# One set of four idle transposes in the gate and up products, where there were three

## The chip, the cores and the metric

The kernel runs on one core of one Trainium2 chip. The metric is the device time of one execution in microseconds (us); the time given for a kernel is the median of several runs.

## What is computed

One encoder block on 512 tokens of width 2048, all in float32: an adaptive norm, a combined input projection, two token mixers side by side (global attention and attention in a window), an output projection, and then a SwiGLU channel mixer with 5632 hidden features and a final norm. The change lies in the channel mixer:

```python
h2 = rms_norm(x, norm2_w[l]) * (1.0 + sc2) + sh2
ff = (jax.nn.silu(h2 @ w_ffn_gate[l]) * (h2 @ w_ffn_up[l])) @ w_ffn_down[l]
x = x + g2 * ff
return rms_norm(x, final_w)
```

## The kernel before

Every float32 product is made of three fp32r matmuls: each operand is split into a high part (ScalarE rounds it, line 135) and a low part (VectorE takes the difference, line 136), and `mm3` (lines 143 to 145) adds high x high, high x low and low x high in PSUM. TensorE's work is therefore a long line of weight loads (128x128) each followed by a matmul.

The program runs the input projection and both mixers first, then `w_out`, and from about 1244 us on the channel mixer, in three stages:

- **Gate and up.** The hidden features are worked in 11 groups of 512 (`for n in range(FU)`, line 1003), in each first `w_gate`, then `w_up`. Except for the first gate group, each is one call of `group7`: a Strassen-like scheme that forms four 512x512 blocks by seven products. It goes over the four blocks of the contraction in the order (2, 3, 0, 1). For each, `wforms` loads 1 MB of weights (SP's queue), makes their sums on VectorE (lines 875 to 878) and splits them into four `whl` tiles; then TensorE makes 84 matmuls of 128x256: seven products in the order 1, 2, 3, 5, 6, 7, 4 (`ORDER`), for each 2 x 2 x 3 matmuls. A group has 336 matmuls. At its end ScalarE and VectorE gather the seven PSUM banks into a tile `c` (lines 932 to 939), gate groups go through SiLU (line 1022), up groups are multiplied with them (line 1025) and stored in DRAM. The weights are prepared ahead of TensorE, by as much as the buffers (`raw`, `whl`) allow.
- **Down, 512 wide.** Two of the hidden groups go through `w_down` by plain products, 128x512 matmuls (about 2120 to 2207 us).
- **Down, 256 wide.** The other groups go through `down_group`, which again has seven products for most of them, with 128x256 matmuls (about 2207 to 2520 us), and a tail of 512-wide products with the final norm.

A *stir* is a call of `stirred` (line 842): four transposes of the 128x128 identity into a PSUM bank that nobody reads. They add nothing to the result. `keep_in_program_order` and `issue_after` (through `after_stir`) pin them: the next matmul of the program is not issued ahead of them. In `group7` a stir stands in front of the second block of the contraction, if the call's argument `stir` is set. Down groups have two of their own: in column block 0 at hidden group 2, and in column block 1 at hidden group 7. So before there are five stirs, 20 transposes: three in gate and up, two in down.

The order of the instructions on each engine is that of the program, with a scheduler that moves instructions by priority where nothing pins them.

Of the kernel before, what the change touches and what calls it, by code (L numbers as in the profile page):

```python
# [89 lines left out]
def encoder_block(ctx: ExitStack, tc, xp, xT, c, ada1_w, ada2_w, b_ada, norm1_w, w_in, q_norm_w, k_norm_w, bias,  # L90
# [33 lines left out]
    def bank(tag):  # L124
        return ps.tile([P, 512], F32, tag=tag, name=tag, bufs={"mm": 4, "S": 2, "T": 1, "Y": 1}[tag])
# [16 lines left out]
    def mm3(o, lh, ll, rh, rl, start, stop, **kw):  # L142
        nc.tensor.matmul(o, lh, rh, start=start, stop=False, **kw)  # L143
        nc.tensor.matmul(o, lh, rl, start=False, stop=False, **kw)  # L144
        nc.tensor.matmul(o, ll, rh, start=False, stop=stop, **kw)  # L145
# [696 lines left out]
    def stirred(b):  # L842

        for o in range(0, 4 * P, P):
            last = behind(nc.tensor.transpose(b[:, o:o + P], ident, ident))
        stir_last.append(last.ins)
# [3 lines left out]
    def after_stir():  # L850
        return tc.issue_after(stir_last.pop()) if stir_last else contextlib.nullcontext()
# [13 lines left out]
    def wforms(w, k0, c0, turned=False, late=False):  # L865
        rt = []
        for a in range(2):
            raw, r3 = unit(w, k0 + 2 * a, 2, c0, 512)
            rt.append((raw, r3[:, :, :256], r3[:, :, 256:]))
        (_, b11, b12), (r1, b21, b22) = rt  # L870
        ta = wq.tile([P, 1024], F32, tag="ta", name="ta", bufs=2)
        tb = wq.tile([P, 1024], F32, tag="tb", name="tb", bufs=1)
        t1, t2_ = (half(ta)[:, a] for a in range(2))
        t3, t4 = (half(tb)[:, a] for a in range(2))
        V.tensor_sub(t1, b12, b11)  # L875
        V.tensor_sub(t2_, b22, t1)  # L876
        V.tensor_sub(t3, b22, b12)
        V.tensor_sub(t4, *((b21, t2_) if turned else (t2_, b21)))
        hl = [wtiles() for _ in range(4)]
        col = lambda e: lambda t: t.rearrange("p (q n) -> p q n", q=2)[:, :, e * 256:(e + 1) * 256]  # L880
        blk = lambda e: lambda t: half(t)[:, e]
        g0 = [t[:, :512].rearrange("p (q n) -> p q n", q=2) for t in hl[0]]
        parts = (b11, (lambda t: t,)), (r1, (col(0), col(1))), (ta, (blk(0), blk(1))), (tb, (blk(0), blk(1)))
        turn = (0, 2, 3, 1) if late else range(4)
        return split7([parts[n] for n in turn], [g0] + hl[1:], [HALVES[n] for n in turn])
# [25 lines left out]
    def group7(wsrc, xs, order, dst, stir=False):  # L911

        bk = {r: bank(BANK[r]) for r in ORDER}
        for n, s in enumerate(order):
            w = wsrc(s)
            if stir and n == 1:
                tp = bank("T")
                stirred(tp)
            for r in ORDER:
                (wh, wl), (xh, xl) = w[r], xs[s][r]  # L920
                for q in range(2):
                    for c in range(2):
                        o = bk[r][:, c * 256:(c + 1) * 256]
                        cs = slice(c * P, (c + 1) * P)
                        first, last = n == 0 and q == 0 and c == 0, n == len(order) - 1 and q == 1
                        with after_stir():
                            mm3(o, wh[:, q, cs], wl[:, q, cs], xh[:, q], xl[:, q], first, last, skip_group_check=True)
        p = {r: b.rearrange("p (c n) -> p c n", c=2) for r, b in bk.items()}
        (d11, d12), (d21, d22) = dst
        with tc.high_priority():  # L930
            p1 = io.tile([P, 512], F32, tag="io", name="p1").rearrange("p (c n) -> p c n", c=2)
            S.activation(p1, p[1], AF.Copy)
            V.tensor_add(d11, p[2], p1)
            V.tensor_add(d21, p[6], p1)
            V.tensor_add(d12, p[5], d21)
            V.tensor_add(d12, p[3], d12)
            V.tensor_add(d21, p[7], d21)
            V.tensor_add(d22, p[5], d21)
            V.tensor_sub(d21, d21, p[4])
# [6 lines left out]
    hx = {}  # L946
# [38 lines left out]
    def c_tile(dt=F32, name="c"):  # L985
        n = next(cn) % 3
        c = (c_p if n else ca).tile([P, 2048], dt, tag=f"c{n}", name=name, bufs=1)
        return c, c.rearrange("p (a t q n) -> p a t q n", a=2, t=2, q=2)
# [9 lines left out]
    def first_pairs():  # L998
        early[0] = ff_pair(0, 0, [wq.tile([P, 1024], F32R, tag="ta", name=f"e0{t}", bufs=2) for t in "hl"], nc.sync)
        e1, _ = c_tile(F32R, "e1")  # L1000
        early[1] = ff_pair(0, 1, [e1[:, :1024], e1[:, 1024:]], nc.sync)

    for n in range(FU):
        cs = []
        for w in (w_gate, w_up):
            c, v = c_tile()
            cs.append(c)
            if n == 0 and w is w_gate:
                for f in range(4):
                    S.activation(v[:, f // 2, :, f % 2], banks[f].rearrange("p (t n) -> p t n", t=2), AF.Silu)  # L1010
                continue
            dst = (v[:, 0, 0], v[:, 1, 0]), (v[:, 0, 1], v[:, 1, 1])

            def wsrc(s):
                d = wforms(w, 4 * s, n * 512)
                if s == 1 and n == FU - 1 and w is w_up:
                    first_pairs()
                return d

            group7(wsrc, hx, (2, 3, 0, 1), dst, w is w_up and n < 3)  # L1020
            if w is w_gate:
                S.activation(c, c, AF.Silu)
        for a in range(2):
            sl = slice(a * 1024, (a + 1) * 1024)
            V.tensor_mul(cs[1][:, sl], cs[1][:, sl], cs[0][:, sl])
        (nc.sync if n < FU - 1 else nc.gpsimd).dma_start(ff_d[n], cs[1])
# [290 lines left out]
```

## Time and profile before

| | us |
|---|---|
| median of 3 runs | 2590.98 |
| lowest and highest run | 2590.06, 2592.19 |
| the profiled execution | 2587.8 |
| its span, first to last instruction | 2585.9 |
| TensorE busy | 2550.0 |
| VectorE busy | 1882.2 |
| ScalarE busy | 1024.5 |

The profile's names: PE is TensorE's matmuls, PEld its weight loads, DVE VectorE, ACT ScalarE, POOL GpSimd, SP SyncE, whose queue issues most loads of weights. A row of the timeline gives the start in us, the duration in us, engine, line, operation, the tile written and the tiles read, the shape, and the count of instructions merged into the row. Matmuls are pipelined: a 128x256 matmul lasts 0.28 us, but the next starts long before it ends, so the rate of work is read from starts, or from the count in a stretch of time, and not from durations. Tiles in the timeline: `whl` is a high or low part of weights, `m0` to `m7`, `x3` and `x56` are parts of the activations, `s` those of the down groups, `T`, `Y`, `S` and `mm` are PSUM banks. L845 is the transposes of a stir, L804 transposes that bring the activations into shape. The stirs of before start at 1303.89, 1380.51, 1457.12, 2211.72 and 2420.26 us.

### The profile page before, as it was taken

What the parts mean: (1) busy time and instruction counts of PE and PEld (TensorE: products, weight loads), DVE (VectorE), ACT (ScalarE), POOL (GpSimd) and SP (SyncE); (2) the same over time, 40 slices, a digit from 0 to 9 for tenths busy, and PEclk for the clock granted to TensorE, in tenths of its full rate; (3) what the DMA queues carried; (4) which work ended last, traced back from release to release, by engine and by line L of the source; (5) the groups of instructions that cost most, each with busy time, mean ns of one, the idle gap of its engine ahead of it and who ended that gap; (6) DMA issues with size and microseconds to landing.
All of it is one profiled execution on the core that took longest, in us unless ns stands there. A gap on an engine that the chain in (4) does not pass through costs nothing.

```text
span 2585.9 us, 40429 instructions
## 1 busy us (share of the span) xinstructions
PE 2550.0 (99%) x16525; PEld 2306.7 (89%) x16525; DVE 1882.2 (73%) x2500; ACT 1024.5 (40%) x1412; POOL 151.4 (6%) x254
## 2 busy tenths in 40 slices
PE   7999999999999999999999999999999999999998
PEld 5888888888888788888999999999999998999996
DVE  8985776456566566556788888787888885777877
ACT  5223554224233332235744444444444454434333
POOL 0100000111111110011000000000000000000010
PEclk8999999999999999999999999999999999999999
DMA  9864234765656876676443343343443446547563
GB/s 353 303 226 145 66 98 166 244 191 169 193 178 198 282 259 220 231 245 211 119 150 118 120 123 123 123 123 99 131 127 119 131 152 222 201 140 241 184 242 113
DMA packets 217466, 457.46 MB, mean 177 GB/s; under 512 B 15056, under 2 KB 68672, under 8 KB 208832
## 3 DMA queue, kind: packets, MB, share of 16 engines
q1 hardware_dynamic: 179728, 307.93, 37.2%
q0 software_dynamic: 29728, 132.20, 15.0%
q10 hardware_dynamic: 7824, 14.74, 1.6%
q8 instruction: 130, 2.13, 0.3%
q14 instruction: 56, 0.46, 0.1%
HBM read 410.74 MB, written 44.07 MB: 176 GB/s over the span
## 4 chain that ended last, share of the span: by engine, by line
PE 91%; DVE 4%; DMA 3%; ACT 1%; issue 1%; SPq 0%; ACTq 0%; DVEq 0%
PE mm L143 19%; PE mm L145 19%; PE mm L144 19%; PE S L143 7%; PE S L145 7%; PE S L144 7%; PE Y L143 3%; PE Y L144 3%; PE Y L145 3%; PE T L145 1%; PE T L144 1%; PE T L143 1%; DMA yr<-y 1%; DMA raw<-in_w_in 1%; DMA raw<-in_w_down 1%
## 5 line engine op out<-in xcount | busy, mean ns | idle before, releaser
L135 ACT ACTIVATE whl<-raw 128x1024 fp32r<-128x1024 f32 (+1 forms) x483 | 463.6, 962 | 855.2 <-PE mm L145 402.9
L136 DVE TENSOR_TENSOR whl<-raw,whl 128x1024 fp32r<-128x1024 f32 (+1 forms) x483 | 531.3, 1109 | 315.2 <-ACT whl L135 314.6
L136 DVE TENSOR_TENSOR whl<-ta,whl 128x1024 fp32r<-128x1024 f32 x104 | 127.3, 1224 | 88.1 <-ACT whl L135 87.8
L135 ACT ACTIVATE whl<-tb 128x1024 fp32r<-128x1024 f32 x104 | 110.5, 1063 | 161.9 <-PE S L145 139.6
L135 ACT ACTIVATE whl<-ta 128x1024 fp32r<-128x1024 f32 x104 | 110.2, 1059 | 153.5 <-PE mm L145 127.6
L308 DVE SCALAR_TENSOR_TENSOR acc<-mw,cact,acc 128x1024 f32<-128x1024 f32 x124 | 158.4, 1278 | 13.6 <-DMA mw<-in_ada_w 13.4
L136 DVE TENSOR_TENSOR whl<-tb,whl 128x1024 fp32r<-128x1024 f32 x104 | 127.0, 1222 | 13.2 <-ACT whl L135 11.2
L286 POOL DMA_DIRECT2D mw<-in_ada_w x112 | 59.8, 534 | 712.0 <-DVE acc L308 416.4
L143 PE MATMUL S<-x56h,whl 128*128 128x256 f32 x336 | 94.4, 281 | 0.4 <-ACT whl L135 0.4
L144 PE MATMUL mm<-x56l,whl 128*128 128x256 f32 x336 | 94.3, 281 | 0.0
L144 PE MATMUL S<-x56l,whl 128*128 128x256 f32 x336 | 94.3, 281 | 0.0
L143 PE MATMUL mm<-x3h,whl 128*128 128x256 f32 x336 | 94.3, 281 | 0.0
L145 PE MATMUL S<-x56h,whl 128*128 128x256 f32 x336 | 94.3, 281 | 0.0
L144 PE MATMUL mm<-x3l,whl 128*128 128x256 f32 x336 | 94.3, 281 | 0.0
L145 PE MATMUL mm<-x56h,whl 128*128 128x256 f32 x336 | 94.3, 281 | 0.0
L145 PE MATMUL mm<-x3h,whl 128*128 128x256 f32 x336 | 94.3, 281 | 0.0
L143 PE MATMUL mm<-x56h,whl 128*128 128x256 f32 x336 | 94.3, 281 | 0.0
L875 DVE TENSOR_TENSOR ta<-raw 128x512 f32<-128x512 f32 x104 | 71.8, 690 | 26.6 <-DMA raw<-in_w_down 24.4
L876 DVE TENSOR_TENSOR ta<-raw,ta 128x512 f32<-128x512 f32 x104 | 71.6, 688 | 25.9 <-DMA raw<-in_w_down 24.3
L143 PE MATMUL mm<-whl,s 128*128 128x256 f32 x320 | 88.8, 277 | 0.0
L145 PE MATMUL mm<-whl,s 128*128 128x256 f32 x320 | 88.6, 277 | 0.0
L144 PE MATMUL mm<-whl,s 128*128 128x256 f32 x320 | 88.6, 277 | 0.0
(1517 smaller groups left out, 8575.6 us busy)
## 6 DMA issues: line engine op xcount, KB each, us to landing
raw<-in_w_in SPq DMA_DIRECT2D x133, 512.0 KB, 4.0
mw<-in_ada_w POOLq DMA_DIRECT2D x112, 512.0 KB, 4.9
raw<-in_w_gate SPq DMA_DIRECT2D x92, 512.0 KB, 3.8
raw<-in_w_up SPq DMA_DIRECT2D x88, 512.0 KB, 3.7
raw<-in_w_down SPq DMA_DIRECT2D x88, 512.0 KB, 5.0
raw<-in_ada_w POOLq DMA_DIRECT2D x29, 1024.0 KB, 6.6
raw<-in_w_out SPq DMA_DIRECT2D x48, 512.0 KB, 5.1
ffd<-c SPq DMA_DIRECT2D x10, 1024.0 KB, 4.8
```

Source lines behind the costliest of these rows:

```text
L135: pin(S.activation(hi, src, AF.Copy))
L136: pin(eng.tensor_sub(lo, src, hi))
L143: nc.tensor.matmul(o, lh, rh, start=start, stop=False, **kw)
L144: nc.tensor.matmul(o, lh, rl, start=False, stop=False, **kw)
L145: nc.tensor.matmul(o, ll, rh, start=False, stop=stop, **kw)
L286: mod["queue"].dma_start(w, ada2_w[n * P:(n + 1) * P, :])
L308: behind(V.scalar_tensor_tensor(acc, part, cact[:, k:k + 1], acc, op0=ALU.mult, op1=ALU.add))
L875: V.tensor_sub(t1, b12, b11)
L876: V.tensor_sub(t2_, b22, t1)
```

## The change

```diff
-            group7(wsrc, hx, (2, 3, 0, 1), dst, w is w_up and n < 3)
+            group7(wsrc, hx, (2, 3, 0, 1), dst, w is w_up and n == 0)
```

The stir in the first up group stays; those in the second and third up groups go, eight transposes in all. The stirs of the down groups stay. Nothing else differs on any engine.

TensorE, in the second up group between the first and the second block of the contraction (`Y` takes the last product of one block, `mm` the first of the next), before:

```order
L144 MATMUL Y_11368<-m5l_7227,whl_11382 128x256
L145 MATMUL Y_11368<-m5h_7226,whl_11382 128x256
L845 MATMUL T_11497<-ident_80 128x128 x4
L143 MATMUL mm_11362<-m6h_7228,whl_11485 128x256
L144 MATMUL mm_11362<-m6l_7229,whl_11485 128x256
```

And at the same place now:

```order
L145 MATMUL Y_11368<-m5h_7226,whl_11382 128x256
L143 MATMUL Y_11368<-m5h_7226,whl_11382 128x256
L144 MATMUL Y_11368<-m5l_7227,whl_11382 128x256
L145 MATMUL Y_11368<-m5h_7226,whl_11382 128x256
L143 MATMUL mm_11362<-m6h_7228,whl_11485 128x256
L144 MATMUL mm_11362<-m6l_7229,whl_11485 128x256
```

The first matmul of the second block follows the last of the first block at once. TensorE at the same place of the third up group, before:

```order
L144 MATMUL Y_12259<-m5l_7227,whl_12273 128x256
L145 MATMUL Y_12259<-m5h_7226,whl_12273 128x256
L845 MATMUL T_12388<-ident_80 128x128 x4
L143 MATMUL mm_12253<-m6h_7228,whl_12376 128x256
L144 MATMUL mm_12253<-m6l_7229,whl_12376 128x256
```

And now:

```order
L145 MATMUL Y_12254<-m5h_7226,whl_12268 128x256
L143 MATMUL Y_12254<-m5h_7226,whl_12268 128x256
L144 MATMUL Y_12254<-m5l_7227,whl_12268 128x256
L145 MATMUL Y_12254<-m5h_7226,whl_12268 128x256
L143 MATMUL mm_12248<-m6h_7228,whl_12371 128x256
L144 MATMUL mm_12248<-m6l_7229,whl_12371 128x256
```

Here too the four transposes are gone and the neighbours close up; the numbers of the tiles alone have shifted.

## The prediction

> **What bounds the kernel now.** I read the page first, for the engine that sets the time; then the waits of TensorE, to see whether anything holds it up in gate and up; then busy time by stages, for the rate at which it works; last the order of instructions in time around each stir.
>
> ```profile
> span 2585.9 us, 40429 instructions
> PE 2550.0 (99%) x16525; PEld 2306.7 (89%) x16525; DVE 1882.2 (73%) x2500; ACT 1024.5 (40%) x1412; POOL 151.4 (6%) x254
> PEclk8999999999999999999999999999999999999999
> PE 91%; DVE 4%; DMA 3%; ACT 1%; issue 1%; SPq 0%; ACTq 0%; DVEq 0%
> ```
>
> TensorE (PE) is busy for 99% of the span and carries 91% of the chain that ended last; its granted clock is full after the first slice. From 1294.2 us to the end the list of its waits holds one row, 1.4 us that end just there, ahead of the first w_up products:
>
> ```profile
> PE mm L143 <- ACT c L1010: 1.4, 1, 1.4
> ```
>
> So from there on the time is a count of matmuls times the spacing from one to the next. That spacing is not one number. Busy time by stage (start:end, its length, then PE busy and in brackets the instructions, weight loads, DVE, ACT, POOL, granted clock, DMA share, GB/s):
>
> ```profile
> 1304.50:1380.40 75.90, 75.90 (x672) 75.90 (x671) 65.32 (x82) 32.97 (x35) 0.00 (x0) 1.00 0.42 128
> 1381.10:1457.00 75.90, 75.90 (x672) 75.90 (x671) 63.95 (x80) 32.97 (x35) 0.00 (x0) 1.00 0.41 124
> 1457.70:2120.40 662.70, 662.70 (x5629) 662.70 (x5628) 538.91 (x664) 282.08 (x297) 1.63 (x3) 1.00 0.40 122
> 2120.50:2207.40 86.90, 86.90 (x385) 71.99 (x384) 54.91 (x61) 39.15 (x48) 7.99 (x15) 1.00 0.67 227
> 2212.30:2420.20 207.90, 207.90 (x1837) 207.90 (x1836) 163.70 (x206) 83.35 (x90) 10.92 (x20) 1.00 0.54 180
> 2420.90:2520.00 99.10, 99.10 (x877) 99.10 (x876) 74.87 (x90) 30.59 (x32) 10.33 (x18) 1.00 0.66 240
> ```
>
> All rows but the fourth hold 128x256 matmuls alone. Of each count about 2.4 were under way when the window began (0.28 us each, at a spacing of 0.115), so the spacings are 75.90/669.6 = 113.35 ns, the same again, then 662.70/5626.6 = **117.78 ns**, and in the last two rows 207.90/1834.6 = 113.32 and 99.10/874.6 = 113.31. Same shape, same clock of 1.00, no wait, and 4.45 ns (3.9%) apart. I call them the 113 pace and the 118 pace. The borders of the windows are the stirs: the third one, at 1457.1, is where 113 turns into 118, and the fourth, in the first down group, is where it turns back. Word for word:
>
> ```profile
> 1457.00 0.28 PE L145 MATMUL Y<-m5h,whl 128*128 128x256 f32 x1
> 1457.12 0.60 PE L845 MATMUL T<-ident 128*128 128x128 f32 x4
> 1457.48 0.37 PE L143 MATMUL mm<-m6h,whl 128*128 128x256 f32 x1
> 1457.68 0.28 PE L144 MATMUL mm<-m6l,whl 128*128 128x256 f32 x1
> 1457.80 0.28 PE L145 MATMUL mm<-m6h,whl 128*128 128x256 f32 x1
> ...
> 1458.27 0.28 PE L143 MATMUL mm<-m6h,whl 128*128 128x256 f32 x1
> ```
>
> ```profile
> 2211.13 0.28 PE L144 MATMUL mm<-whl,s 128*128 128x256 f32 x1
> ...
> 2211.60 0.28 PE L145 MATMUL mm<-whl,s 128*128 128x256 f32 x1
> 2211.72 0.60 PE L845 MATMUL T<-ident 128*128 128x128 f32 x4
> 2212.07 0.37 PE L143 MATMUL mm<-whl,s 128*128 128x256 f32 x1
> 2212.27 0.28 PE L144 MATMUL mm<-whl,s 128*128 128x256 f32 x1
> ...
> 2212.74 0.28 PE L145 MATMUL mm<-whl,s 128*128 128x256 f32 x1
> ...
> 2213.19 0.28 PE L143 MATMUL mm<-whl,s 128*128 128x256 f32 x1
> ```
>
> After the third stir five steps take 0.59 us (118 each) and it stays so for 663 us. After the fourth the first four steps take 0.47 (118 each) and the next four 0.45 (113): the pace settles within half a microsecond, one way or the other, and then keeps. The first stir found 118 and left 113; the second found 113 and left it:
>
> ```profile
> 1303.42 0.28 PE L145 MATMUL Y<-m5h,whl 128*128 128x256 f32 x1
> ...
> 1303.77 0.28 PE L145 MATMUL Y<-m5h,whl 128*128 128x256 f32 x1
> 1303.89 0.60 PE L845 MATMUL T<-ident 128*128 128x128 f32 x4
> ...
> 1380.39 0.28 PE L145 MATMUL Y<-m5h,whl 128*128 128x256 f32 x1
> 1380.51 0.60 PE L845 MATMUL T<-ident 128*128 128x128 f32 x4
> 1380.86 0.37 PE L143 MATMUL mm<-m6h,whl 128*128 128x256 f32 x1
> 1381.07 0.28 PE L144 MATMUL mm<-m6l,whl 128*128 128x256 f32 x1
> ```
>
> (1303.42 to 1303.77 is three steps, 117 each.) In short, the trace shows a pace that four transposes can change in either direction, and that nothing else in gate and up changes.
>
> **The change part by part.** It removes eight transposes and moves nothing; every other instruction of every engine stands in its old order.
>
> *The stirs themselves.* Around the second, from the last matmul before it to the second one after it is 1381.07 - 1380.39 = 0.68 us, where two steps of the 113 pace take 0.23: it costs 0.45 us. The third costs 1457.68 - 1457.00 - 0.23 = 0.45. All of it is on TensorE's path. Together **0.9 us** less.
>
> *The pace after the third stir.* Up to the second stir program and order are those of before, so the first stir should again leave the 113 pace. Without the second and third there is then no transpose until 2211 to end it. 5626.6 matmuls x 4.45 ns = **25.0 us** less, if the pace keeps over the remaining 8 up groups and 8 gate groups. For that: the two 75.90 us windows at 113 hold the seams of four groups (evacuation, SiLU, product, store) and the 207.90 us window the seams of down groups, and neither lost the pace; the 662.70 us row shows no change the other way.
>
> *What would be late next.* A quicker TensorE could run into its suppliers. It already ran at 113 for 152 us with these suppliers: DVE was busy 65.32 of 75.90 us (86%), DMA 0.42. The tightest place that I found in such a stretch is the second weight set of a gate group, behind the DVE's evacuation of the up group before (DVE rows first, then TensorE's first use):
>
> ```profile
> 1337.16 2.35 DVE L1025 TENSOR_TENSOR c<-c 128x1024 f32<-128x1024 f32 x2
> 1339.43 1.82 DVE L136 TENSOR_TENSOR whl<-raw,whl 128x512 fp32r<-128x512 f32 x2
> ...
> 1342.42 0.28 PE L143 MATMUL mm<-m6h,whl 128*128 128x256 f32 x1
> ```
>
> The two splits end at 1341.25, and the first of them (0.69 us long, as its other 128x512 work) at about 1340.1: 2.3 us ahead of its use. A pair of gate and up groups repeats the same work, so I cost this at nothing; were the cover gone, each of the 8 remaining pairs could lose up to a DVE split (1.2 us), 10 us in all, and only if 2.3 us of lead vanish.
>
> *What follows gate and up.* The 512-wide down products (2120.5 to 2207.4) run at 86.90/384 = 226 ns (384 weight loads). Whether their spacing depends on the earlier pace no row shows, as they were entered from 118 alone; twice the 113 pace is 226.6, so they can hardly gain, and at twice 118 they would lose 3.4 us (384 x 8.9 ns). I take nothing. Behind them the kernel before was at 118 until the fourth stir (2211.13 to 2211.60 above is four steps, 118 each), and I expect the same entry. The fourth and fifth stirs then decide the last 307 us as before, or not: below.
>
> The Trainium skill, "TensorE: Matmul & The Clock Gate", section "Wait — 56ns, not 53.3ns?", gives warm back-to-back matmuls one start-to-start time, the columns over 2.4 GHz plus about 2.5 ns (by that page an estimate of 109.2 ns for 256 columns), the same whatever went before. By it no pace is there to be kept, and only the stirs' own time would go. The rows above have two spacings at one granted clock, 113.3 and 117.8, so here the measurement decides, and the sum goes by the rows.
>
> Sum: 25.0 + 0.9 = 25.9 us. The profiled execution took 2587.8 us (span 2585.9 and 1.9 around it), so 2561.9 for its like. The three timed runs have a median of 2590.98, 3.2 above the profiled one and 2.1 apart among themselves. Taken off the median: **2565.1 us**.
>
> **The rivals.** How often does a set of four transposes leave the 118 pace? Besides the five stirs there are eight sets of token transposes (L804) among 128x256 matmuls between 1258 and 1281 us. First and last of the eight stretches behind them:
>
> ```profile
> 1259.20:1261.10 1.90, 1.90 (x19) 1.90 (x18) 1.30 (x2) 1.21 (x3) 0.00 (x0) 1.00 0.76 245
> ...
> 1281.50:1291.40 9.90, 9.90 (x90) 9.90 (x89) 9.90 (x14) 7.70 (x13) 0.00 (x0) 1.00 0.38 108
> ```
>
> Of the stretches between, each holds 18 to 20 matmuls in 1.8 or 1.9 us. 1.90/16.6 = 114 and 9.90/87.6 = 113.0: the 113 pace. With the stirs that is 12 of 13 that left 113, and one that left 118.
>
> 1. *A later stir lands on the 118 pace.* The fourth and the fifth now come some 26 us earlier, against another background of DMA. If the fourth fails, 1834.6 x 4.45 = 8.2 us are given back, 2573.3; if the fifth, 874.6 x 4.45 = 3.9, 2569.0. At 1 in 13 each that is 15%; both stand in unchanged surroundings on TensorE, so 12%.
>
> 2. *The first stir lands on the 118 pace, and nothing mends it.* This one ends slower than before. Place: 1304.2 us. Price: both 75.90 us windows go to 118, 2 x 669.6 x 4.45 = 6.0 us, less the 0.9 of the stirs: +5.1, 2596.1. It decides as soon as the first stir ends at 118 in a timed run. Against it: the profile has it at 113, and all before it is unchanged. For it: timed runs are 3.2 us above the profiled one, about what one 75.90 us window at 118 would add (3.0), so that in them the first stir might fail already and the second mend it. Then the change would come out at -0.9 + 3.0 = +2.1, 2593.1. 10% for both, half each.
>
> 3. *The 113 pace gets lost on its own in gate and up*, at one of the 16 remaining group seams, and without a stir stays lost: anything from 2565.1 to 2593.1, in the middle 2579. In favour: 113 has been watched for 76 us at a stretch there, and 208 us in down, never for 660. 5%.
>
> 4. *The pace does not hang on the stirs* but on something that happened to change at 1457: then only 0.9 us goes, 2590.1, no change. Against it stands that all three changes of pace quoted above, at 1304, 1457 and 2212, fall on a stir to within a microsecond. 3%.
>
> **How the numbers follow.** The forecast has what is left, 70%: 2565.1. Its own range is 2561.5 to 2567, from the 3.2 us between profiled and timed and the runs' spread. With the first rival (up to 2573.3, and a spread of 1.1) the range 2561.5 to 2574.5 holds 82%. About 0.2% (5.2 us) is what a measurement of this kernel can tell from no change. Faster by more: 70 + 12 + 4 of the third rival = 86%. Within: 1 + 5 (the half of the second rival that ends at +2.1) + 3 = 9%. Slower: the other half, which lies at that limit, 5%.
>
> **What would show it.** Right: one stretch from 1304.5 to about 2094.5 us with 113.3 ns spacing and no border at 1380 or 1457; matmuls there at 277 ns mean; no wait of TensorE behind 1294; the 512-wide products at 226; 118 only in the few microseconds ahead of the fourth stir. Wrong: 118 behind 1304 (second rival), a border at a seam of groups (third), 118 from about 1457 with no transpose there (fourth), 118 behind the fourth or fifth stir (first), or waits for `whl` at the second weight set of gate groups.

## The result and the profile after

The changed kernel took 2563.95 us (median of 4 runs, 2560.47 to 2568.16), the kernel before 2591.59 in the same job (4 runs, 2590.06 to 2592.26): a ratio of 0.9895, 95% interval 0.9878 to 0.9912. The profiled execution took 2564.67 us. The page of the changed kernel, its span, TensorE's busy time and clock:

```profile
span 2562.9 us, 40413 instructions
PE 2527.7 (99%) x16517; PEld 2283.7 (89%) x16517; DVE 1880.1 (73%) x2500; ACT 1024.3 (40%) x1412; POOL 151.9 (6%) x254
PEclk8999999999999999999999999999999999999999
```

Busy time of the changed kernel by stage, with the same columns as before; the windows lie between stirs and changes of matmul shape:

```profile
1304.30:2094.20 789.90, 789.90 (x6972) 789.90 (x6971) 668.12 (x825) 348.70 (x367) 1.64 (x3) 1.00 0.41 127
2094.30:2181.30 87.00, 87.00 (x386) 71.96 (x385) 54.79 (x61) 39.21 (x48) 8.01 (x15) 1.00 0.68 228
2186.20:2385.80 199.60, 199.60 (x1763) 199.60 (x1763) 154.44 (x196) 78.64 (x85) 10.93 (x20) 1.00 0.55 183
2394.90:2507.70 112.80, 112.80 (x960) 112.80 (x960) 79.80 (x94) 33.65 (x35) 10.36 (x18) 1.00 0.66 243
```

With the 2.4 matmuls under way taken off each count, all of gate and up behind the first stir now runs at 789.90/6969.6 = 113.3 ns, without a border at 1380 or 1457. The 512-wide stage, now entered from 113, takes 87 us as before. The stretch behind the fourth stir is at 113.4, and the last one, behind the fifth stir, at 112.80/957.6 = **117.8**: in this execution the fifth stir changed 113 into 118, as the third did before. TensorE's instructions around it, after the change:

```profile
2393.73 0.28 PE L144 MATMUL mm<-whl,s 128*128 128x256 f32 x1
...
2394.18 0.28 PE L145 MATMUL mm<-whl,s 128*128 128x256 f32 x1
2394.30 0.60 PE L845 MATMUL T<-ident 128*128 128x128 f32 x4
2394.65 0.36 PE L143 MATMUL mm<-whl,s 128*128 128x256 f32 x1
2394.85 0.28 PE L144 MATMUL mm<-whl,s 128*128 128x256 f32 x1
...
2395.56 0.28 PE L144 MATMUL mm<-whl,s 128*128 128x256 f32 x1
```

Four steps in 0.45 us ahead of it (113 each), six in 0.71 behind it (118).

### The profile page after: what moved, and what is told of

It is laid out like the page before. It is cut to its first block, busy times and chain, and to the rows that moved or that the text cites. A ratio compares the mean times of both kernels' runs of the same rounds, so it can differ in the third digit from the quotient of the medians.

```text
span 2562.9 us, 40413 instructions
## 1 busy us (share of the span) xinstructions
PE 2527.7 (99%) x16517; PEld 2283.7 (89%) x16517; DVE 1880.1 (73%) x2500; ACT 1024.3 (40%) x1412; POOL 151.9 (6%) x254
## 4 chain that ended last, share of the span: by engine, by line
PE 92%; DVE 3%; DMA 2%; ACT 1%; issue 1%; SPq 0%; ACTq 0%; DVEq 0%
PE mm L145 19%; PE mm L143 19%; PE mm L144 19%; PE S L143 7%; PE S L145 7%; PE S L144 7%; PE Y L143 3%; PE Y L144 3%; PE Y L145 3%; PE T L145 1%; PE T L144 1%; PE T L143 1%; DMA yr<-y 1%; DMA raw<-in_w_in 1%; PE T L591 1%
## 5 line engine op out<-in xcount | busy, mean ns | idle before, releaser
L143 PE MATMUL S<-x56h,whl 128*128 128x256 f32 x336 | 92.9, 276 | 0.5 <-ACT whl L135 0.5
L143 PE MATMUL mm<-x3h,whl 128*128 128x256 f32 x336 | 92.8, 276 | 0.0
L144 PE MATMUL mm<-x3l,whl 128*128 128x256 f32 x336 | 92.8, 276 | 0.0
L145 PE MATMUL mm<-x3h,whl 128*128 128x256 f32 x336 | 92.8, 276 | 0.0
L143 PE MATMUL mm<-x56h,whl 128*128 128x256 f32 x336 | 92.8, 276 | 0.0
L144 PE MATMUL mm<-x56l,whl 128*128 128x256 f32 x336 | 92.8, 276 | 0.0
L145 PE MATMUL mm<-x56h,whl 128*128 128x256 f32 x336 | 92.8, 276 | 0.0
L145 PE MATMUL S<-x56h,whl 128*128 128x256 f32 x336 | 92.8, 276 | 0.0
L144 PE MATMUL S<-x56l,whl 128*128 128x256 f32 x336 | 92.8, 276 | 0.0
L143 PE MATMUL mm<-whl,s 128*128 128x256 f32 x320 | 88.9, 278 | 0.0
L144 PE MATMUL mm<-whl,s 128*128 128x256 f32 x320 | 88.7, 277 | 0.0
L145 PE MATMUL mm<-whl,s 128*128 128x256 f32 x320 | 88.7, 277 | 0.0
```

## The experiments

The first question was whether a stir changes the pace at all, the second why one stir ends at 113 and another at 118. Where a ratio is given it is against the kernel before in the same job. In these jobs the kernel before turned out to have two times: 50 of its 96 executions (the four beside the result included) lie between 2564.5 and 2570.2 us, 46 between 2585.7 and 2597.9, and nothing between. The shares differ from job to job: 16 of 31 near 2567 in the first, then 9 of 29, 6 of 9 and 19 of 23; all four of the runs beside the result were near 2590. A median says little of such a kernel, so the single times are told.

**No stir in gate and up.**

```diff
-            group7(wsrc, hx, (2, 3, 0, 1), dst, w is w_up and n == 0)
+            group7(wsrc, hx, (2, 3, 0, 1), dst, False)
```

> No stir in gate and up; the two of the down groups stay. Theory (a set of transposes sets the pace, and nothing else in gate and up changes it): 118 ns spacing from the first up group at about 1294 us to the 512-wide products, 6972 matmuls x 4.45 ns = 31 us more than the changed kernel less 0.45 for the stir, about 2594.5 us. Rival (the pace changes by other things, the stirs only happened to lie near): 113 for most of the stretch, about 2564.

Ten executions: six from 2561.0 to 2567.8, four from 2594.2 to 2596.6. The profile is of one of the four. Two windows, first just behind the wait at the first up group, then the rest of gate and up:

```profile
1296.50:1299.40 2.90, 2.90 (x16) 2.90 (x16) 2.90 (x4) 2.69 (x4) 0.00 (x0) 0.50 0.68 194
1299.60:2127.60 828.00, 828.00 (x7032) 828.00 (x7032) 675.88 (x834) 351.14 (x369) 1.64 (x3) 1.00 0.38 122
```

828.00/7029.6 = 117.8 ns from end to end, as the theory has it: without a stir nothing ended that pace in 828 us. But the theory took it for granted that the first up group begins at 118, and in six executions of ten the time is that of 113 throughout. Behind the 1.4 us wait either pace can begin. In this execution the clock was at half for 3 us there as well; that happens in six of the fourteen profiles of this study and goes with either pace.

**Half of the change: the third stir taken out, the second kept.**

```diff
-            group7(wsrc, hx, (2, 3, 0, 1), dst, w is w_up and n == 0)
+            group7(wsrc, hx, (2, 3, 0, 1), dst, w is w_up and n < 2)
```

> Stirs in the first and second up groups, the third taken out: half of the change. Theory: the third stir was the whole loss, so 113 from 1304 to the 512-wide products, 0.45 us above the changed kernel, about 2564.5. If the second stir's landing is chance, 1 in 13 that it leaves 118: 2589. Rival (the pace is lost at a time near 1457 whatever stands there): 2589 in every run.

Six executions from 2561.1 to 2566.6, four from 2591.1 to 2594.4. The profile, of one of the six:

```profile
1306.90:1382.70 75.80, 75.80 (x671) 75.80 (x670) 64.89 (x81) 32.90 (x35) 0.00 (x0) 1.00 0.38 125
1383.50:2097.20 713.70, 713.70 (x6300) 713.70 (x6299) 602.25 (x743) 315.31 (x332) 1.64 (x3) 1.00 0.39 127
```

113.4 and 113.3. There is no bad time near 1457 us: without a stir the pace is kept. But by the times the second stir (or the first) ends at 118 in 4 of 10, not in 1 of 13.

**The other half: the second stir taken out, the third kept.**

```diff
-            group7(wsrc, hx, (2, 3, 0, 1), dst, w is w_up and n == 0)
+            group7(wsrc, hx, (2, 3, 0, 1), dst, w is w_up and n in (0, 2))
```

> Stirs in the first and third up groups, the second taken out: the other half. Theory with chance landings (1 in 13 at 118): the third stir most likely leaves 113, about 2564.5 us. Theory with a fixed bad place (something at the third up group makes the landing 118 there): 2590.5, 0.45 below the kernel before, in every run.

Four from 2564.4 to 2566.3, six from 2587.0 to 2592.3. The profile, of one of the four, ahead of and behind the third group's stir:

```profile
1307.70:1459.70 152.00, 152.00 (x1344) 152.00 (x1342) 129.91 (x162) 66.25 (x70) 0.00 (x0) 1.00 0.39 127
1460.50:2098.00 637.50, 637.50 (x5628) 637.50 (x5627) 537.52 (x663) 281.96 (x297) 1.64 (x3) 1.00 0.39 127
```

Here the stir in the third up group leaves 113 (637.50/5625.6). So it is no bad place either; by the times it ends at 118 in six of the ten executions.

**The third stir alone.**

```diff
-            group7(wsrc, hx, (2, 3, 0, 1), dst, w is w_up and n == 0)
+            group7(wsrc, hx, (2, 3, 0, 1), dst, w is w_up and n == 2)
```

> Only the stir in the third up group. Theory: 118 from 1294 to about 1463 us, where the stir comes; 1344 matmuls x 4.45 = 6.0 us above the changed kernel, 2570, if it lands at 113; 2594.5 if it lands at 118. A fixed bad place gives 2594.5 in every run, chance gives 2570 in most.

Nine of ten are near the low time: five from 2562.6 to 2564.7, four from 2568.8 to 2572.3; one took 2593.9. The profile is one of the four:

```profile
1298.00:1463.60 165.60, 165.60 (x1408) 165.60 (x1408) 137.23 (x171) 68.87 (x73) 0.00 (x0) 1.00 0.39 125
1464.50:2102.00 637.50, 637.50 (x5627) 637.50 (x5627) 537.17 (x662) 281.93 (x297) 1.63 (x3) 1.00 0.39 127
```

118 (165.60/1405.6) up to the stir, 113 behind it. By the times, the same stir that ends at 118 in six of ten executions behind another stir does so in one of ten when the pace it meets is left to the entry. From here the theory was: a stir that meets 118 leaves 113; one that meets 113 leaves either.

**The changed kernel in more executions, and without the fifth stir.** The first has no edit against the changed kernel; the second is

```diff
-        down_group(cc, (6, 7), cl, acc, late(cc), () if cc else (8, 9), stir=7 if cc == 1 else None, late=cc > 1,
+        down_group(cc, (6, 7), cl, acc, late(cc), () if cc else (8, 9), stir=None, late=cc > 1,
```

> The changed kernel itself, in more executions. So far the kernel before ended near 2568 in 16 of 35 executions and near 2590 in 19; the changed one near 2564 in 4 of 4. Theory A (a stir met at 118 leaves 113, a stir met at 113 leaves either; the first stir meets 118 in some 4 of 10 executions): near 2564 in three quarters or more, the rest near 2593. Theory B (each stir lands at 118 in about half of the executions whatever it meets): near 2564 in half, near 2593 in half.

> The changed kernel without the second stir of the down groups, the one that meets 113. Theory A: the stretch behind it keeps 113 in every execution in which the fourth stir left it, 0.45 us less everywhere and 4.3 less where the fifth used to fail: a median 1 to 4 us below the changed kernel of the same job. Rival (each stretch loses the pace by itself in time): no gain, the profile shows 118 in the last stretch as often as before.

The changed kernel: 12 of 12 from 2560.3 to 2567.6, median 2564.62, ratio 0.9932 (0.9902 to 0.9961). Without the fifth stir: ten from 2560.1 to 2565.4 and two at 2593.4 and 2594.5, median 2563.09, ratio 0.9945 (0.9906 to 0.9984). In gate and up the two programs are alike, so by the times the first stir failed in 2 of 28 executions (with the four of the result). The profile without the fifth stir is of one of these two:

```profile
1305.20:2126.10 820.90, 820.90 (x6972) 820.90 (x6972) 669.53 (x826) 348.56 (x367) 1.63 (x3) 1.00 0.38 122
2419.20:2535.80 116.60, 116.60 (x1031) 116.60 (x1030) 86.56 (x102) 37.90 (x40) 10.33 (x18) 1.00 0.67 244
```

The first stir left 118 (820.90/6969.6 = 117.8), the very event that the prediction priced at 2596.1. The last stretch, without a stir of its own, kept the 113.4 that the fourth had left, through a wait of 0.8 us. Theory B, half of the executions near 2593 whatever a stir meets, is out. The gain from leaving the fifth out is 1.6 us between the means of the executions that are not near 2590 (2562.7 and 2564.3); with standard deviations of 2.1 and 2.5 us over 10 and 16 executions that is not clear of chance.

**A stir in every group.**

```diff
-            group7(wsrc, hx, (2, 3, 0, 1), dst, w is w_up and n == 0)
+            group7(wsrc, hx, (2, 3, 0, 1), dst, True)
```

> A stir in all 21 groups of gate and up that group7 does. Its own time is 20 x 0.45 = 9 us more. Theory A: in the profile each stir that meets 118 leaves 113, and of those that meet 113 a part leaves 118, so that stretches of 118 are one group long (336 matmuls x 4.45 = 1.5 us each). Theory B: 118 follows 118 as often as it follows 113. With half of the stirs at 113 failing, a third of the groups at 118: 7 x 1.5 + 9 = 20 us above the changed kernel, 2584; with none failing 2573.

2581.51 us, and this time all eight executions lie together, 2579.9 to 2585.4. The stretches behind the first eight of 21 stirs, one group each:

```profile
1305.20:1343.00 37.80, 37.80 (x336) 37.80 (x335) 32.79 (x42) 15.43 (x17) 0.00 (x0) 1.00 0.33 109
1343.70:1383.00 39.30, 39.30 (x336) 39.30 (x335) 32.00 (x41) 17.20 (x18) 0.00 (x0) 1.00 0.42 134
1383.80:1421.60 37.80, 37.80 (x336) 37.80 (x335) 31.39 (x40) 15.38 (x17) 0.00 (x0) 1.00 0.33 105
1422.30:1460.10 37.80, 37.80 (x336) 37.80 (x335) 31.45 (x40) 17.10 (x18) 0.00 (x0) 1.00 0.44 139
1460.80:1500.10 39.30, 39.30 (x336) 39.30 (x335) 32.44 (x41) 15.39 (x17) 0.00 (x0) 1.00 0.33 106
1500.90:1538.60 37.70, 37.70 (x335) 37.70 (x334) 30.75 (x39) 17.04 (x18) 0.00 (x0) 1.00 0.42 137
1539.40:1577.20 37.80, 37.80 (x336) 37.80 (x335) 31.75 (x41) 15.40 (x17) 0.00 (x0) 1.00 0.33 106
1577.90:1617.20 39.30, 39.30 (x336) 39.30 (x336) 31.91 (x41) 17.18 (x18) 0.00 (x0) 1.00 0.42 137
```

The same 336 matmuls take 37.8 us or 39.3: 113, 118, 113, 113, 118, 113, 113, 118, and so on to the 21st, 7 of them at 118. That is no chance. Every stir that meets 118 leaves 113 (7 of 7), and of two that meet 113 the first keeps it and the second ends it. So the 113 pace seems to have at least two forms, which look alike in their spacing, and a stir carries one over into the next. 7 x 1.5 + 9 us above the changed kernel's mean of 2564.3 gives 2583.8, 2.3 us above what was measured.

**Stirs of three, one and two transposes in every group.**

```diff
-        for o in range(0, 4 * P, P):
+        for o in range(0, 3 * P, P):
```

(and `P` or `2 * P`, on top of the edit above.)

> A stir of three transposes in every group, where four gave a strict cycle: one group at 118, two at 113. Theory C (what counts is how far the stir shifts the stream against its period of three matmuls, four transposes shifting it by one): three transposes shift it by none, so the pace of the first groups stays to the end, all 113 (about 2561 + 20 x 0.34 = 2568) or all 118 (about 2597). Rival D (any interruption acts alike, whatever its length): the cycle of three again, 7 groups at 118, 2568 + 7 x 1.5 = 2578.

> A stir of one transpose in every group. Theory C: one is four less three, so the cycle of one group at 118 and two at 113 comes back, 2561 + 20 x 0.13 + 7 x 1.5 = 2574. Rival E (a longer stir is needed to change the pace at all): the pace of the first groups stays to the end, 2564 or 2593.

> A stir of two transposes in every group. Theory C: the cycle of three runs the other way round, 7 groups at 118 again, 2561 + 20 x 0.24 + 7 x 1.5 = 2576. Rival: no cycle, either pace kept.

Three transposes: 2569.5, 2571.1 and 2576.5 us. First and last whole group in the profile, which is of the slowest of the three (its last stretch of the down groups, 948 matmuls, ran at 118):

```profile
1308.10:1346.00 37.90, 37.90 (x337) 37.90 (x336) 32.99 (x42) 15.49 (x17) 0.00 (x0) 1.00 0.34 109
...
2038.20:2076.10 37.90, 37.90 (x337) 37.90 (x336) 31.75 (x41) 17.18 (x18) 0.00 (x0) 1.00 0.43 140
```

113 behind all 21. One transpose: six executions from 2593.9 to 2600.1, none lower; ahead of the first stir, behind it, and in the last whole group:

```profile
1300.90:1307.00 6.10, 6.10 (x56) 6.10 (x55) 5.49 (x7) 2.13 (x2) 0.00 (x0) 1.00 0.49 158
1307.60:1346.70 39.10, 39.10 (x334) 39.10 (x333) 33.48 (x43) 15.68 (x17) 0.00 (x0) 1.00 0.34 107
...
2061.70:2100.90 39.20, 39.20 (x335) 39.20 (x334) 31.55 (x41) 17.45 (x18) 0.00 (x0) 1.00 0.41 134
```

113.8 ahead of the first stir, which ended it (39.10/331.6 = 117.9); behind the other 20, which all met 118, it is 118 too. So rival E, whose 2593 fits the time, falls: one transpose changed the pace. In the down groups the same single transposes left 113, where the fourth stir met 118 and where the fifth met 113:

```profile
2223.00:2429.00 206.00, 206.00 (x1820) 206.00 (x1820) 163.77 (x206) 81.76 (x89) 10.91 (x20) 1.00 0.54 182
2431.00:2530.00 99.00, 99.00 (x876) 99.00 (x875) 73.83 (x88) 30.34 (x32) 9.81 (x17) 1.00 0.66 242
```

Two transposes: 2575.6 to 2579.4 us, 113 behind all 21 in gate and up, and then this behind the fourth and the fifth stir:

```profile
2195.30:2411.10 215.80, 215.80 (x1835) 215.80 (x1834) 165.83 (x208) 83.28 (x90) 11.42 (x21) 1.00 0.52 176
2411.80:2520.20 108.40, 108.40 (x959) 108.40 (x958) 75.88 (x90) 32.53 (x34) 9.81 (x17) 1.00 0.68 252
```

117.8 and 113.3: two transposes left 118 where they met it once and 113 once. The expected 2576 was met by luck: not 7 groups of gate and up (10.5 us) but the stretch behind the fourth stir (8.2 us) ran at 118. In gate and up the rival (no cycle, the pace kept) held. Theory C, a count of transposes modulo three, falls: it has three right, but one and two wrong. Rival D falls with it, since the length of a stir decides what it does. What stands is that in gate and up each length carries the pace over in a way of its own: four in a cycle of three, three and two always onto 113 where they met 113, one onto 118 the one time it met 113 and the 20 times it met 118.

**Two candidates.** Both leave out the fifth stir. The first has three transposes in the first up group, the second four there and three in the next gate group.

```diff
-            group7(wsrc, hx, (2, 3, 0, 1), dst, w is w_up and n == 0)
+            group7(wsrc, hx, (2, 3, 0, 1), dst, 3 if w is w_up and n == 0 else 0)
```

```diff
-            group7(wsrc, hx, (2, 3, 0, 1), dst, w is w_up and n == 0)
+            group7(wsrc, hx, (2, 3, 0, 1), dst, 4 if w is w_up and n == 0 else 3 if w is w_gate and n == 1 else 0)
```

(`stirred` takes the number of transposes that `group7` was given.)

> A candidate: the one stir of the first up group with three transposes, the second stir of the down groups left out. Theory (a set of three met at 113 always leaves 113, as 20 of 20 did): executions that come to the first stir at 113 all end near 2561; those that come at 118 go on at 118 or not, which no run has shown in gate and up, near 2561 or 2593. If it mends all, the median is near 2561.5 with none near 2593; if it mends none, some 4 in 10 are near 2593. Rival (the landing is chance whatever the size): 1 in 14 near 2593, as with four transposes.

> A candidate: a stir of four transposes in the first up group, then one of three in the next gate group to mend a failed first one, the second stir of the down groups left out. Theory (three never break 113, and may mend 118): near 2561.5 in all but 1 in 28 executions, 0.34 us more than with the first stir alone. Rival (a second set, met at 113, breaks it as often as the second one of four did): 4 in 10 near 2592.

Three alone: eleven from 2560.4 to 2566.6, one at 2595.1, ratio 0.9984 (0.9955 to 1.0013), as the rival has it (1 in 14). The profile is of one of the eleven and met 113 at the stir, so how the theory fares at 118 is not shown. Four and then three: 12 of 12 from 2560.6 to 2568.8, median 2563.87, ratio 0.9972 (0.9949 to 0.9996) in a job where the kernel before was near 2567 in 19 of 23. The second candidate's profile behind its second stir, and behind the fourth stir to the end of the down groups:

```profile
1344.00:2095.80 751.80, 751.80 (x6635) 751.80 (x6635) 634.41 (x783) 332.97 (x350) 1.64 (x3) 1.00 0.40 127
2188.00:2504.50 316.50, 316.50 (x2795) 316.50 (x2795) 242.48 (x298) 116.90 (x125) 21.29 (x38) 1.00 0.58 205
```

113.3 in both (751.80/6632.6 and 316.50/2792.6). The rival (4 in 10 near 2592) is out. Whether three transposes mend a failed first stir was not met in a profile; in the down groups of the run with three everywhere they left 113 where they met 118 at the fourth stir, and 118 where they met it at the fifth, so they do not always mend. Against the changed kernel (16 of 16 near 2564) no difference can be claimed.

## Why the prediction was right, and where it was not

*Two paces, set by stirs: shown.* Where a stir stands the pace may change, and between stirs it stayed, 118 for up to 828 us and 113 for 790, through all seams of gate and up. The third rival (113 lost on its own) came up there in none of the fourteen profiles; once, with stirs of three, a down group went from 113 to 118 behind a wait of 0.9 us, while waits of 0.4 to 0.8 us at that place in three other profiles left 113. The fourth rival (the pace does not hang on the stirs) is excluded by the cycle with a stir in every group. What would be late next was nothing: no wait of TensorE in gate and up at 113, as the 2.3 us of lead said.

*The sum: right between the two profiled executions.* From the first stir to the 512-wide stage, 2120.42 - 1303.89 before and 2094.26 - 1303.65 after: 816.53 and 790.61, which is 25.9 less, as summed. The fifth stir then cost 957.6 x 4.45 = 4.3 us, of which the last stage gave back 1.3 (from its first matmul to the end of the span 56.4 before, 55.1 after), and the spans differ by 23.0. The first rival named this event with 3.9.

*The step that failed: "the pace after the third stir" as a property of the kernel before.* The prediction took it that the third stir always ends at 118, from one profile and four close times. By the times it, or another, does so in 46 of 96 executions; in the other 50 the kernel before runs near 2567 and the change has little to gain: the means of its low executions and of the 16 of the changed kernel are 2567.3 and 2564.3. The 25 us are the price of an event, and the change takes away the event. Over all executions the means are 2578.2 and 2564.3, 13.9 us apart; in the one job with many of both 2583.3 and 2564.3. How often the event comes in a given job is what decides the measured ratio, and the profile of one execution can't show it. So the close hit has luck in it: all four executions of the kernel before beside the result were near 2590, and beside the last job's 23, whose mean is 2570.8, the same change would have shown 6.5 us. That the timed runs lay 3.2 us above the profiled one is in the range of what the fifth stir does (4.3) and of what passes ahead of gate and up, where the end of the 1.4 us wait lies between 1293.5 and 1298.7 us in the fourteen profiles; it was not traced further.

The cycle of the experiment with a stir in every group would explain the two times. If the kernel before comes in at 118, its three stirs leave 113, 113 and 118, as profiled; if it comes in at 113, they leave 113, 118 and 113, which costs one stretch of 3.0 us and the two stirs' 0.9, and the two means are 3.0 apart. This is not shown: no low execution of the kernel before was profiled, and with the third stir taken out the profile came in at 113 and kept it behind both stirs.

*The odds of a stir: wrong in kind.* "12 of 13" lumped together stirs that meet 118 and stirs that meet 113. Counted over all profiles for stirs of four transposes, those that met 118 left 113 in 22 of 23, those that met 113 kept it in 19 of 29. Hence the change is good for another reason than fewer throws of a die: gate and up are entered at 118 in 6 of 14 profiles, which the first stir mended in three of the four profiles that have both, and the fourth meets 118 in every one; the second, which the change takes out, meets what the first left, nearly always 113, and can there only harm, and the third can at best mend what the second broke. The first stir at 118 without repair (second rival, 10%) came in 2 of 28, at 2593.4 and 2594.5.

*Left open.* What in TensorE makes the two paces and the forms of 113 was not found. The weight loads differ. Those of the third matmul of `mm3` (L145), then of the second (L144), kernel before, at 118 behind the third stir, in ns as min/median/max:

```profile
L145 PEld LDWEIGHTS mm<-x3h,whl x268: 191/192/193, 1460.5 to 2114.5; 128*128 128x128 f32 x134
```

```profile
L144 PEld LDWEIGHTS mm<-x3l,whl x268: 187/188/188, 1460.4 to 2114.4; 128*128 128x128 f32 x134
```

And the same load of L145 in the kernel before at 113:

```profile
L145 PEld LDWEIGHTS mm<-x3h,whl x64: 187/188/188, 1307.2 to 1451.5; 128*128 128x128 f32 x64
```

At 118 one weight load of each three takes 4 ns longer, but not always that of L145. Ahead of the fourth stir it is that of L144 in all fourteen profiles; here in the kernel before, then L145 ahead of the fifth stir of the run with two transposes:

```profile
L144 PEld LDWEIGHTS mm<-whl,s x11: 191/192/193, 2207.8 to 2211.4; 128*128 128x128 f32 x11
```

```profile
L145 PEld LDWEIGHTS mm<-whl,s x19: 192/192/192, 2400.1 to 2410.7; 128*128 128x128 f32 x19
```

So the 118 pace has forms too, and what a stir leaves goes with the form that it meets. Four transposes that met the slow load at L144 left 113 in 14 of 14 profiled cases, at L145 in 8 of 9. One transpose left 113 where it met L144 and 118 in the 20 cases with L145 or L143; two left 118 where they met L144 and 113 where they met L145, so what looked like a toss there need not be one. Three steps at 118 are 13.3 ns more than three at 113. Why, no run here tells.

## What to carry to other kernels

Where an engine is busy to the last per cent, compare its rate stage by stage: a border between two rates with no wait, the same shapes and the same clock is time that no busy share shows. Before a single profile is explained, time the kernel often enough, in several jobs, to see whether it has one time or two; a change that only alters the odds looks like a large gain or like nothing, by the job. And an instruction that can mend a state can also break it: place it where the bad state is known to come in, not wherever it once helped.

## What the runs showed of the hardware

- Entering 128x256 matmuls from 512-wide ones gave the 118 pace in every profile (14 of 14 ahead of the fourth stir); entering them behind a 1.4 us wait gave 118 in 6 and 113 in 8.
- In 6 of 14 profiles TensorE's clock fell to half for 3.4 us just behind that wait (0.50 in the row of the first experiment), after about 1.8 us with two matmuls in them. The Trainium skill, "TensorE: Matmul & The Clock Gate", section "Part 1: The HAM clock gate", ties the fall to an idle window of some 3.4 us; here it came behind a shorter pause, which all fourteen profiles have, in some executions and not in others.
- The length of an interruption by idle transposes, and the pace and form that it met, went with the rate of the hundreds of matmuls behind it: in gate and up 118 stood behind each of 21 single transposes of 0.27 us (113 met once, 118 met 20 times) and 113 behind each of 21 sets of three (113 met each time); in the down groups a single transpose left 113 twice.
